# Weight remainders on GpSimd, a fourth landing buffer and a reordered first stage in a two-layer hybrid decoder

## The chip, the cores and the metric

The kernel runs on one core of a Trainium2 chip. The metric is the time of one execution on the device, in microseconds (us). TensorE (PE in the rows) multiplies matrices, VectorE (DVE), ScalarE (ACT) and GpSimd (POOL) do element-wise work, and SyncE (SP) issues most DMAs. SBUF is the on-chip working memory and PSUM holds the results of matmuls.

## The reference

Two layers (DEPTH = 2) over 512 positions of width 1024. Each layer normalises its input, scales and shifts it with a conditioning vector, and multiplies it with one wide input matrix. Two token mixers use the result: a sparse attention with 128 selected keys per query, and a chunked state-space scan. Both are projected, merged by gates, multiplied with an output matrix and added to the input.

```python
def _layer(x, c, w_ada, b_ada, norm_g, w_in, ...):
    mod = jax.nn.silu(c) @ w_ada + b_ada
    shift, scale, gate = jnp.split(mod, 3, axis=-1)
    h = _rmsnorm(x, norm_g) * (1.0 + scale[:, None, :]) + shift[:, None, :]
    proj = h @ w_in
    ...
    y_att = (o_att * jax.nn.silu(g_att)) @ w_branch_a
    ...
    y_ssd = y @ w_branch_s
    merged = jax.nn.sigmoid(gl_att) * y_att + jax.nn.sigmoid(gl_ssd) * y_ssd
    return x + gate[:, None, :] * (merged @ w_out)
```

All of it is fp32.

## The kernel before

**Weights in two parts.** TensorE works on the type fp32r here, which keeps fewer bits than fp32, so every operand of the large products is split: a rounded part `hi` and a remainder `lo = value - hi`. A product is three matmuls: hi by hi, hi by lo and lo by hi. Class `W` streams the weights in tiles of 128x1024 (some 128x936 or 128x512). `W.load` issues the DMA from SP into a landing buffer `raw`, of which there are RAWB = 3. `W.split` casts `raw` to `whi` on ScalarE (L194) and subtracts on VectorE to get the remainder `wlo` (L195). There are WB = 3 pairs of `whi` and `wlo`. `W.get` keeps AHEAD = 3 tiles split in front of the one in use and asks for RAWB more loads. There are 130 such tiles in the execution.

Some entries of the same stream are tiles of the conditioning matrix (`ada`). They land in `raw` too, and `ada_block` (L149) multiplies them on VectorE with the conditioning vector `cb` and sums along the rows. All VectorE instructions stand in one queue and run in order.

**The first stage.** `x` comes in four pieces. VectorE and ScalarE square it, and TensorE sums the squares over the channels with matmuls on a constant (`mones`, L301) into two PSUM tiles, one for each half of the 512 positions. Then `pre0(k)` runs for the eight channel tiles k = 0 to 7 of `tok_section`. For k = 0, half by half, it forms the reciprocal root (L263 to L267), then `h` (L312 on VectorE), its rounded part `hh` (L313 on ScalarE) and its remainder `hl` (L315 on VectorE). For each further k it adds two `ada` tiles (L149, for the scale and the shift), `h` and `hl` over all positions, and the split of one weight tile. `chain` ties the VectorE instructions of this stage into one fixed row.

`tok_section` runs, for each k, four blocks of 128 positions times a weight tile: three matmuls for the key and index columns (468 wide, the K part) and three for the query columns (512 wide, the Q part, one step later).

**The later stages.** The key part is rotated (`rope_k`) while the Q part ends. Then `block` multiplies weight tiles with `hh` and `hl` over all 512 positions, 24 matmuls to a tile, while other work is interleaved by generators: the index scores and the selection of keys, the scan (`ssd`), and attention. GpSimd has little to do: 16 multiplications of 128x768 in `ssd` (L715) and some DMAs, among them the loading of `x` for the residual (L881) and its saving between the layers (L912). In `out_step` the output product runs in two halves of the positions, and the second layer's `hh` and `hl` are made from the first half while the second half is still multiplied. The second layer's K part is then run for blocks 0 and 1, and after that for blocks 2 and 3.

The order within each engine's queue comes from the tile framework, which places instructions by their priority as their inputs are expected; `tc.high_priority(W_PRIO)` moves the split forward. A queue is strictly in order: what stands behind a waiting instruction waits too.

Of the kernel before, what the change touches and what calls it, by code (L numbers as in the profile page):

```python
# [12 lines left out]
AF = mybir.ActivationFunctionType  # L13
OP = mybir.AluOpType
# [4 lines left out]
KT = D // 128  # L19
# [14 lines left out]
LAG = 1  # L34
# [5 lines left out]


W_PRIO = 2000
RAWB = 3
TMPB = 7
WB = 3
AHEAD = 3
# [1 line left out]
MG_PRIO = 2300  # L48
P_ACT = 1
WARM = 1  # L50
ORDER = "s0 s1 s2 s3 T b0 b1 b2 b3 x0 x1 x2 x3 x4 x5 x6 x7 I S g0 g1 z0 z1 g2 z2 z3 g3 z4 z5 g4 z6 z7 g5 N0 g6 g7"
R_INDEX = 1
R_TOPK_X = 0.1
# [9 lines left out]
def trunk(ctx, tc, x, c, wk, wq, wt, wa, ada, pk, cst, out):  # L63
# [15 lines left out]
    def scratch(dt=F32):  # L79
        return tmp.tile([128, 512], dt, name="tmp", tag="tmp", bufs=TMPB)  # L80
# [7 lines left out]
    def raw(ap):  # L88
        return ap.bitcast(F32)
# [66 lines left out]
    class W:  # L156
        def __init__(self):
            self.src, self.loaded, self.ready, self.cb = [], {}, {}, None
            self.late, self.extra, self.keep, self.ahead = 10 ** 9, None, {}, AHEAD

        def add(self, ap, n):
            self.src.append((ap, n, None))
# [12 lines left out]
                sp.dma_start(r[:, :n], ap)  # L175
                self.loaded[i] = r

        def split(self, i, link=lambda ins: None):
            if i in self.ready:
                return  # L180
            self.load(i)
            _, n, mod = self.src[i]
            r = self.loaded[i]
            if mod is not None:
                ada_block(*mod, self.cb, r)
                self.ready[i] = None
                return
            if i in self.keep:
                hi, lo = self.keep[i]
            else:  # L190
                hi = wp.tile([128, 1024], F32R, name="whi", tag="whi", bufs=WB)
                lo = wp.tile([128, 1024], F32R, name="wlo", tag="wlo", bufs=WB)
            with tc.high_priority(W_PRIO):
                act.copy(hi[:, :n], r[:, :n])  # L194
                link(dve.tensor_sub(lo[:, :n], r[:, :n], raw(hi[:, :n])))  # L195
            self.ready[i] = (hi, lo)

        def get(self, i):
# [51 lines left out]
    def block(i, n, rh, rl, out, cols=slice(0, L)):  # L250
        hi, lo = w.get(i)
        for k in range(n):
# [4 lines left out]
            if k % 2:  # L257
                yield

    def rstd_from(r, sums, count, newton, link=lambda ins: None):  # L260
        n = r.shape[-1]
        if newton:
            act.activation(r, sums, AF.Abs_reciprocal_sqrt, bias=epst, scale=-2.0)  # L263
            t = scratch()[:, :n]
            act.activation(t, r, AF.Square)
            link(dve.scalar_tensor_tensor(t, sums, -0.5 * EPS, t, op0=OP.add, op1=OP.mult))
            link(dve.scalar_tensor_tensor(r, t, 1.5, r, op0=OP.add, op1=OP.mult))  # L267
# [25 lines left out]
    for k in range(0, KT, 2):  # L293
        if k < 4:
            in_row(act.activation(*silu[k // 2], AF.Silu))
        sq, sq1 = scratch(), scratch()
        in_row(act.activation(sq, xt[:, k], AF.Square))
        chain(dve.tensor_mul(sq1, xt[:, k + 1], xt[:, k + 1]))
        chain(dve.tensor_add(sq, sq, sq1))
        for cols, s in zip(HALVES, sums):  # L300
            pe.matmul(s, mones, sq[:, cols], start=k == 0, stop=k == KT - 2)  # L301
    pool.dma_start(cbs[:], cb[:1])
    for l in range(DEPTH):
        chain(dve.scalar_tensor_tensor(gb[l], par(l, P_BA + 8, 8), 1.0, par(l, P_NG, 8), op0=OP.add, op1=OP.mult))
# [14 lines left out]
    for l in range(DEPTH):  # L319
# [42 lines left out]
            w.ahead = 1  # L362
        accK = [bank(t) for t in BK.split()]

        def tok_section(parts, blocks, pre):
            got = {}
            for step in range(KT + max(p[3] for p in parts)):
                if step < KT:
                    pre(step)
                for i, (ids, n, acc, lag) in enumerate(parts):  # L370
                    k = step - lag
                    if not 0 <= k < KT:
                        continue
                    if k % 2 == 0:
                        got[i] = w.get(ids[k // 2])
                    a, b = (t[:, k % 2 * n:(k % 2 + 1) * n] for t in got[i])
                    for t in blocks:
                        ts = slice(t * 128, (t + 1) * 128)
                        pe.matmul(acc[t][:, :n], hh[:, k, ts], a, start=k == 0, stop=False)  # L379
                        pe.matmul(acc[t][:, :n], hh[:, k, ts], b, start=False, stop=False)  # L380
                        pe.matmul(acc[t][:, :n], hl[:, k, ts], a, start=False, stop=k == KT - 1)  # L381
                yield

        def pre0(k):
            if k == 0:
                for cols, s in zip(HALVES, sums):
                    rstd_from(rst[:, cols], s, D, True, chain)
                    h = make_h(0, k, cols, chain)
                    next(h)
                    if cols.start == 0:  # L390
                        w.split(ids0[0], chain)
                        w.load(ids0[3])
                    for _ in h:
                        pass
            else:
                h = make_h(0, k, slice(0, L), chain)
                next(h)
            if k + 1 < KT:
                ada_block(0, 9 + k, cb, aws[2 * k + 3], chain)
            for _ in h:  # L400
                pass
            if k + 1 < KT:
                ada_block(0, k + 1, cb, aws[2 * k + 2], chain)
                w.split(ids0[k + 1], chain)
                if k + 4 < KT:
                    w.load(ids0[k + 4])
                    load_ada(k + 4)

        if l == 0:
            accQ = [bank(t) for t in BQ.split()]  # L410
            rest = tok_section([(ids_k[0], NKS, accK, 0), (ids_q, 512, accQ, LAG)], range(NB), pre0)
# [597 lines left out]
```

## Time and profile before

| | us |
|---|---|
| median of 3 runs | 924.59 (923.75 to 925.49) |
| the profiled execution | 926.5 |
| span of its trace | 924.7 |
| TensorE busy | 906.5 (98%) |
| VectorE busy | 703.9 (76%) |
| ScalarE busy | 521.0 (56%) |
| GpSimd busy | 49.6 (5%) |

The span goes from the first to the last instruction; 1.8 us of the profiled execution lie around it. Busy time of TensorE counts modelled ends of pipelined matmuls, so 98% does not say that every matmul starts as early as it could: how far apart the matmuls start is read from the timeline. The granted clock of TensorE has two levels, 1.2 and 2.4 GHz, and stands in the rows as a share of the higher one.

### The profile page before, as it was taken

How to read it: one execution, taken by the hardware profiler on the slowest of the kernel's cores; microseconds unless marked ns; L12 is line 12 of the kernel's file. 1: busy time of each engine (PE TensorE's matmuls, PEld its weight loads, DVE VectorE, ACT ScalarE, POOL GpSimd, SP SyncE). 2: the span in 40 equal slices, each digit the busy share in tenths (PEclk: the TensorE clock that was granted, in tenths of full speed). 3: DMA queues.
4: the chain of work that ended last, by engine and by line, in shares of the span. 5: the costliest groups of instructions: out<-in, count | busy, mean ns of one | idle time of the engine just before them, and what ended most of it. 6: DMA issues, size and time to landing. Idle time of an engine off the chain costs nothing.

```text
span 924.7 us, 13016 instructions
## 1 busy us (share of the span) xinstructions
PE 906.5 (98%) x4780; PEld 743.8 (80%) x4780; DVE 703.9 (76%) x1384; ACT 521.0 (56%) x946; POOL 49.6 (5%) x53
## 2 busy tenths in 40 slices
PE   8999999999999999999999999999999999999996
PEld 4887788888887877777998878888888878778895
DVE  7987999999775765678497699999984675455834
ACT  5457894386265754535365588745653775463433
POOL 0000110031000000000000001102210000000000
PEclk8999999999999999999999999999999999999999
DMA  9832433232346432687344225234323532334502
GB/s 357 317 114 69 164 111 103 103 137 84 102 139 200 138 133 72 220 282 266 96 134 140 89 93 180 94 98 131 125 66 117 169 117 91 92 122 149 207 24 91
DMA packets 40609, 128.05 MB, mean 138 GB/s; under 512 B 4417, under 2 KB 6721, under 8 KB 40546
## 3 DMA queue, kind: packets, MB, share of 16 engines
q1 hardware_dynamic: 36162, 111.43, 36.6%
q0 software_dynamic: 4384, 15.80, 4.9%
q8 instruction: 37, 0.61, 0.3%
q14 instruction: 26, 0.21, 0.1%
HBM read 118.76 MB, written 8.46 MB: 138 GB/s over the span
## 4 chain that ended last, share of the span: by engine, by line
PE 88%; DVE 5%; DMA 4%; ACT 1%; issue 1%; SPq 0%; DVEq 0%; ACTq 0%
PE mm L254 21%; PE mm L255 21%; PE mm L256 21%; PE av L826 2%; PE tr L821 2%; DMA raw<-ada 2%; DVE wlo L195 1%; PE qk L723 1%; PE mm L379 1%; PE mm L381 1%; PE mm L380 1%; PE qk L798 1%; PE qk L799 1%; DMA raw<-wt 1%; PE av L740 1%
## 5 line engine op out<-in xcount | busy, mean ns | idle before, releaser
L254 PE MATMUL mm<-H,whi 128*128 128x512 f32 x640 | 258.6, 404 | 0.0
L256 PE MATMUL mm<-H,wlo 128*128 128x512 f32 x640 | 251.4, 393 | 0.0
L255 PE MATMUL mm<-H,whi 128*128 128x512 f32 x640 | 251.2, 393 | 0.0
L195 DVE TENSOR_TENSOR wlo<-raw,whi 128x1024 fp32r<-128x1024 f32 (+2 forms) x130 | 158.0, 1215 | 56.6 <-ACT whi L194 54.7
L194 ACT CAST whi<-raw 128x1024 fp32r<-128x1024 f32 (+2 forms) x130 | 130.3, 1003 | 113.1 <-PE mm L255 84.7
L254 PEld LDWEIGHTS mm<-H,whi 128*128 128x128 f32 x640 | 120.6, 188 | 26.3 <-issue 3.9
L256 PEld LDWEIGHTS mm<-H,wlo 128*128 128x128 f32 x640 | 120.5, 188 | 25.6 <-issue 0.3
L255 PEld LDWEIGHTS mm<-H,whi 128*128 128x128 f32 x640 | 120.7, 189 | 24.4 <-issue 1.9
L581 DVE MAX8 m<-B 128x8 f32<-128x256 f32 (+2 forms) x96 | 53.1, 554 | 1.2
L603 DVE SCALAR_TENSOR_TENSOR tmp<-mm,prm,tmp 128x511 f32<-128x511 f32 (+2 forms) x72 | 52.8, 736 | 0.0
L582 DVE MATCH_REPLACE8 B<-m,B 128x256 f32<-128x256 f32 (+2 forms) x96 | 52.0, 541 | 0.0
L254 PE MATMUL mm<-X,whi 128*128 128x512 f32 x128 | 51.6, 403 | 0.0
L256 PE MATMUL mm<-X,wlo 128*128 128x512 f32 x128 | 50.2, 392 | 0.3 <-DVE wlo L195 0.3
L803 ACT ACTIVATE S<-S,mx 128x128 f32<-128x128 f32 (+3 forms) x64 | 35.5, 556 | 25.3 <-DVE mx L801 25.2
L149 DVE SCALAR_TENSOR_TENSOR raw<-raw,KI 128x1024 f32<-128x1024 f32 x20 | 24.5, 1223 | 31.5 <-DMA raw<-ada 31.4
L712 ACT ACTIVATE X<-X,acs 128x128 f32<-128x128 f32 x128 | 40.5, 390 | 0.1
L255 PE MATMUL mm<-G,whi 128*128 128x512 f32 x96 | 37.7, 393 | 0.2 <-DVE G L870 0.2
L254 PE MATMUL mm<-S,A 128*128 128x256 f32 x128 | 36.9, 289 | 0.0
L256 PE MATMUL mm<-S,C 128*128 128x256 f32 x128 | 36.2, 283 | 0.0
L898 DVE SCALAR_TENSOR_TENSOR X<-mm,mod,X 128x256 f32<-128x256 f32 (+1 forms) x24 | 13.7, 571 | 28.5 <-PE mm L256 28.5
L822 ACT COPY B<-tr 128x512 f32<-128x512 f32 x40 | 22.7, 583 | 20.9 <-PE tr L821 20.6
L715 POOL TENSOR_TENSOR S<-S,G 128x768 f32<-128x768 f32 x16 | 31.1, 1954 | 60.8 <-ACT G L604 31.2
(269 smaller groups left out, 1766.0 us busy)
## 6 DMA issues: line engine op xcount, KB each, us to landing
raw<-wt SPq DMA_DIRECT2D x103, 512.0 KB, 3.5
raw<-ada SPq DMA_DIRECT2D x20, 512.0 KB, 3.9
X<-AD POOLq DMA_DIRECT2D x16, 512.0 KB, 4.4
raw<-wk SPq DMA_DIRECT2D x12, 468.0 KB, 3.4
B<-ada SPq DMA_DIRECT2D x9, 512.0 KB, 4.4
raw<-wq SPq DMA_DIRECT2D x8, 512.0 KB, 3.9
gsave<-tmp SPq DMA_DIRECT2D x16, 256.0 KB, 2.4
tmp<-gsave SPq DMA_DIRECT2D x16, 256.0 KB, 4.0
```

The lines of the kernel that those rows point to most:

```text
L149: link(dve.scalar_tensor_tensor(w, w, 1.0, cb, op0=OP.mult, op1=OP.mult, accum_out=m))
L194: act.copy(hi[:, :n], r[:, :n])
L195: link(dve.tensor_sub(lo[:, :n], r[:, :n], raw(hi[:, :n])))
L254: pe.matmul(out, h, rh[:, k, cols], start=k == 0, stop=False)
L255: pe.matmul(out, h, rl[:, k, cols], start=False, stop=False)
L256: pe.matmul(out, lw, rh[:, k, cols], start=False, stop=k == n - 1)
L581: dve.max(m8, sc)
L582: dve.match_replace(sc, m8, sc, GONE)
L603: dve.scalar_tensor_tensor(cc[:, i:], p[:, :L - i], cw(3 - i), cc[:, i:], op0=OP.mult, op1=OP.add)
L712: act.activation(ab[:, h, i], ab[:, h, i], AF.Relu, scale=-1.0, bias=acs[:, 2 * kt + h, i:i + 1])
L715: pool.tensor_tensor(cs_, cs_, BC[:, 2 + g, 128:].rearrange("p (c l) -> p c l", c=3)[:, None] .to_broadcast([128, 2, 3, 128]), op=OP.mult)
L803: act.activation(PP[:, e, :n], PP[:, e, :n], AF.Exp, bias=mx[:, e:e + 1], scale=-1.0, accum_out=sums_[:, e:e + 1])
```

## The change

- Every remainder `wlo` is subtracted on GpSimd instead of VectorE, and `W.lows` remembers the instruction. The three kinds of tiles, 128x1024, 128x936 and 128x512, all move.
- RAWB goes from 3 to 4: a fourth landing buffer.
- `rstd_from` is divided into `root` (the two ScalarE steps) and `corrected` (the two VectorE steps). In `pre0(0)` both halves' roots come first, then both halves' `h`, then both remainders `hl`.
- In `tok_section` the three matmuls of a block are no longer next to each other. First all blocks run on the rounded weights, with `hh` and `hl`, then all blocks run on the remainder. For k = 0 the row is fixed with dependencies that cost no wait.
- Behind the sums three matmuls on a tile of ones, 128x512 and fp32, run into a bank that nobody reads (IDLE = 3).
- The four DMAs that load `x` for the residual stand in GpSimd's queue behind the remainder of the last branch tile (`a7`).

```diff
-RAWB = 3
+RAWB = 4
+IDLE = 3
...
                 act.copy(hi[:, :n], r[:, :n])
-                link(dve.tensor_sub(lo[:, :n], r[:, :n], raw(hi[:, :n])))
+                self.lows[i] = pool.tensor_sub(lo[:, :n], r[:, :n], raw(hi[:, :n]))
...
-            pe.matmul(s, mones, sq[:, cols], start=k == 0, stop=k == KT - 2)
+            summed = pe.matmul(s, mones, sq[:, cols], start=k == 0, stop=k == KT - 2)
+    for i in range(IDLE):
+        made = pe.matmul(warm.rearrange("p (a b) -> p a b", a=4), ones, ones[:, None, :].to_broadcast([128, 4, 128]),
+                         start=True, stop=True)
+        tc.add_manual_dep(made.ins, summed.ins.name, NOSYNC)
+        summed = made
...
-                        pe.matmul(acc[t][:, :n], hh[:, k, ts], a, start=k == 0, stop=False)
-                        pe.matmul(acc[t][:, :n], hh[:, k, ts], b, start=False, stop=False)
-                        pe.matmul(acc[t][:, :n], hl[:, k, ts], a, start=False, stop=k == KT - 1)
+                        for h in (hh, hl):
+                            made = pe.matmul(acc[t][:, :n], h[:, k, ts], a, start=k == 0 and h is hh, stop=False)
...
+                    for t in blocks:
+                        pe.matmul(acc[t][:, :n], hh[:, k, t * 128:(t + 1) * 128], b, start=False, stop=k == KT - 1)
...
-                for cols, s in zip(HALVES, sums):
-                    rstd_from(rst[:, cols], s, D, True, chain)
-                    h = make_h(0, k, cols, chain)
+                sides = [(rst[:, cols], s) for cols, s in zip(HALVES, sums)]
+                ts = [root(*side) for side in sides]
+                hs = [make_h(0, k, cols, chain) for cols in HALVES]
+                for side, t, h in zip(sides, ts, hs):
+                    corrected(*side, t, chain)
...
-            pool.dma_start(xt[:, 2 * j:2 * j + 2], x[:, 2 * j:2 * j + 2] if l == 0 else xsave[:, 2 * j:2 * j + 2])
+            made = pool.dma_start(xt[:, 2 * j:2 * j + 2], x[:, 2 * j:2 * j + 2] if l == 0 else xsave[:, 2 * j:2 * j + 2])
+            tc.add_manual_dep(made.ins, w.lows[ids_m["a7"]].ins.name, NOSYNC)
```

What this does to the queues is seen in the order of the built programs. Numbers in the names tell buffers apart; line numbers are those of the kernel that the row belongs to.

VectorE before, from the first `h` of the first stage to the middle of step 1 (`H0` and `H1` hold `hh` and `hl`; `C` and `S` hold `ada` tiles; `G1` is `cb`):

```order
L312 SCALAR_TENSOR_TENSOR tmp_191<-X_85,gsc0_116,rst_120 128x256
L195 TENSOR_TENSOR wlo_195<-raw_166,whi_194 128x936
L315 SCALAR_TENSOR_TENSOR H1_164<-tmp_191,mod0_114,H0_163 128x256
L266 SCALAR_TENSOR_TENSOR tmp_202<-tr_123,tmp_202 128x256
L267 SCALAR_TENSOR_TENSOR rst_120<-tmp_202,rst_120 128x256
L312 SCALAR_TENSOR_TENSOR tmp_206<-X_85,gsc0_116,rst_120 128x256
L315 SCALAR_TENSOR_TENSOR H1_164<-tmp_206,mod0_114,H0_163 128x256
L149 SCALAR_TENSOR_TENSOR C_80,mod0_114<-C_80,G1_76 128x1024 x2
L195 TENSOR_TENSOR wlo_215<-raw_168,whi_214 128x1024
L312 SCALAR_TENSOR_TENSOR tmp_234<-X_85,gsc0_116,rst_120 128x512
```

Every step has one remainder of a weight tile in VectorE's row. The same piece of VectorE's queue after:

```order
L324 SCALAR_TENSOR_TENSOR tmp_197<-X_85,gsc0_116,rst_120 128x256
L269 SCALAR_TENSOR_TENSOR tmp_193<-tr_123,tmp_193 128x256
L270 SCALAR_TENSOR_TENSOR rst_120<-tmp_193,rst_120 128x256
L324 SCALAR_TENSOR_TENSOR tmp_208<-X_85,gsc0_116,rst_120 128x256
L327 SCALAR_TENSOR_TENSOR H1_167<-tmp_197,mod0_114,H0_166 128x256
L327 SCALAR_TENSOR_TENSOR H1_167<-tmp_208,mod0_114,H0_166 128x256
L150 SCALAR_TENSOR_TENSOR C_80,mod0_114<-C_80,G1_76 128x1024 x2
L324 SCALAR_TENSOR_TENSOR tmp_237<-X_85,gsc0_116,rst_120 128x512
```

The remainders are gone from VectorE and the halves of k = 0 are interleaved. They stand in GpSimd's queue, here from the first stage on, after:

```order
L197 TENSOR_TENSOR wlo_201<-raw_169,whi_200 128x936
L197 TENSOR_TENSOR wlo_218<-raw_171,whi_217 128x1024
L197 TENSOR_TENSOR wlo_246<-raw_175,whi_245 128x936
L197 TENSOR_TENSOR wlo_286<-raw_204,whi_285 128x1024
L197 TENSOR_TENSOR wlo_326<-raw_221,whi_325 128x936
L197 TENSOR_TENSOR wlo_366<-raw_249,whi_365 128x1024
L197 TENSOR_TENSOR wlo_402<-raw_289,whi_401 128x936
L197 TENSOR_TENSOR wlo_438<-raw_329,whi_437 128x1024
```

These eight belong to the first stage, which gave GpSimd nothing to do before.

TensorE after, from the end of the sums to the K part's pass on the remainder for k = 0:

```order
L308 MATMUL tr_123<-tmp_148,mones_103 128x256
L310 MATMUL mm_108<-ones_94 128x512 x3
L392 MATMUL qk_181<-whi_200,H0_166 128x468
L392 MATMUL qk_181<-whi_200,H1_167 128x468
L392 MATMUL qk_182<-whi_200,H0_166 128x468
L392 MATMUL qk_182<-whi_200,H1_167 128x468
L392 MATMUL mm_183<-whi_200,H0_166 128x468
L392 MATMUL mm_183<-whi_200,H1_167 128x468
L392 MATMUL mm_184<-whi_200,H0_166 128x468
L392 MATMUL mm_184<-whi_200,H1_167 128x468
L399 MATMUL qk_181<-wlo_201,H0_166 128x468
```

Before, the second matmul of the K part already took the remainder `wlo`; now it is the ninth, and the second takes `hl` (`H1`).

## Rows read from the trace of the kernel before

**Rows 1.** The page, parts 1 and 2: busy time, and TensorE's granted clock.
```profile
PE 906.5 (98%) x4780; PEld 743.8 (80%) x4780; DVE 703.9 (76%) x1384; ACT 521.0 (56%) x946; POOL 49.6 (5%) x53
PEclk8999999999999999999999999999999999999999
```

**Rows 2.** Windows: stretch, PE, PEld, DVE, ACT, POOL busy (instructions), granted clock, DMA share, GB/s.
```profile
15.00:20.00 5.00, 3.65 (x8) 2.58 (x9) 4.32 (x9) 2.74 (x5) 0.00 (x0) 0.60 1.03 414
20.00:25.00 5.00, 5.00 (x18) 3.99 (x17) 5.00 (x9) 2.38 (x5) 0.00 (x0) 0.71 0.93 332
...
40.00:45.00 5.00, 5.00 (x24) 4.27 (x24) 5.00 (x9) 2.05 (x4) 0.00 (x0) 1.00 1.03 402
...
285.00:290.00 5.00, 5.00 (x18) 4.01 (x18) 3.58 (x12) 3.16 (x10) 0.00 (x0) 0.66 0.45 115
...
480.00:485.00 5.00, 5.00 (x25) 4.42 (x24) 5.00 (x10) 3.87 (x11) 0.00 (x0) 1.00 0.67 201
```

**Rows 3.** Timeline, first stage: start, duration, engine, line, operation [idle before <-releaser].
```profile
12.92 0.59 PE L301 MATMUL tr<-tmp,mones 128*128 128x256 f32 x2
...
15.13 0.48 DVE L312 SCALAR_TENSOR_TENSOR tmp<-X,gsc,rst 128x256 f32<-128x256 f32 x1
...
16.35 0.76 PE L379 MATMUL qk<-whi,H 128*128 128x468 f32 x1 [2.83 <-ACT H L313]
...
19.44 1.22 DVE L149 SCALAR_TENSOR_TENSOR C<-C,G 128x1024 f32<-128x1024 f32 x1
...
20.39 0.59 PE L379 MATMUL mm<-whi,H 128*128 128x468 f32 x1
...
20.78 0.59 PE L380 MATMUL mm<-wlo,H 128*128 128x468 f32 x1
```

**Rows 4.** Timeline of VectorE, one step of the first stage.
```profile
41.15 1.22 DVE L195 TENSOR_TENSOR wlo<-raw,whi 128x1024 fp32r<-128x1024 f32 x1
42.29 0.74 DVE L312 SCALAR_TENSOR_TENSOR tmp<-X,gsc,rst 128x512 f32<-128x512 f32 x1
...
45.91 1.12 DVE L195 TENSOR_TENSOR wlo<-raw,whi 128x936 fp32r<-128x936 f32 x1
```

**Rows 5.** Timeline, end of the first stage: VectorE's last remainder, TensorE's last steps.
```profile
53.30 0.75 DVE L315 SCALAR_TENSOR_TENSOR H<-tmp,mod,H 128x512 fp32r<-128x512 f32 x1 [0.85 <-ACT H L313]
...
54.40 0.37 PE L379 MATMUL qk<-whi,H 128*128 128x468 f32 x1
...
56.96 0.40 PE L379 MATMUL tr<-whi,H 128*128 128x512 f32 x1
...
62.46 0.46 PE L466 MATMUL qk<-identr,B 128*128 128x128 f32 x4
```

**Rows 6.** Timeline, GpSimd's multiplications and VectorE's instructions beside them.
```profile
186.81 3.67 POOL L715 TENSOR_TENSOR S<-S,G 128x768 f32<-128x768 f32 x2
...
188.39 3.19 DVE L195 TENSOR_TENSOR wlo<-raw,whi 128x1024 fp32r<-128x1024 f32 x1
...
202.05 1.83 POOL L715 TENSOR_TENSOR S<-S,G 128x768 f32<-128x768 f32 x1 [0.18 <-ACT S L709]
...
202.62 0.73 DVE L747 SCALAR_TENSOR_TENSOR C<-C,prm,av 128x512 f32<-128x512 f32 x1
```

**Rows 7.** Timeline, start of attention in the first layer.
```profile
277.42 0.33 SPq L175 DMA_DIRECT2D raw<-ada  x1
...
282.84 1.23 DVE L149 SCALAR_TENSOR_TENSOR raw<-raw,KI 128x1024 f32<-128x1024 f32 x1 [2.91 <-DMA raw<-ada]
...
284.33 0.33 PE L798 MATMUL qk<-KK,A 128*128 128x128 f32 x1 [2.02 <-DVE mx L801]
```

**Rows 8.** Chain that ended last, in order of time: start, duration, link.
```profile
10.85 0.85 PE av L301 x2
...
418.44 9.18 DMA raw<-wt
...
427.70 1.05 ACT A L194
```

More of the change, by code (lines that the diff above doesn't have):

```diff
@@ L159, in __init__ @@
             self.late, self.extra, self.keep, self.ahead = 10 ** 9, None, {}, AHEAD
+            self.lows = {}
         def add(self, ap, n):
@@ L176, in load, with split @@
                 self.loaded[i] = r
-        def split(self, i, link=lambda ins: None):
+        def split(self, i):
             if i in self.ready:
@@ L258, in block, with root, corrected @@
                 yield
+    def root(r, sums):
+        act.activation(r, sums, AF.Abs_reciprocal_sqrt, bias=epst, scale=-2.0)
+        t = scratch()[:, :r.shape[-1]]
+        act.activation(t, r, AF.Square)
+        return t
+    def corrected(r, sums, t, link=lambda ins: None):
+        link(dve.scalar_tensor_tensor(t, sums, -0.5 * EPS, t, op0=OP.add, op1=OP.mult))
+        link(dve.scalar_tensor_tensor(r, t, 1.5, r, op0=OP.add, op1=OP.mult))
     def rstd_from(r, sums, count, newton, link=lambda ins: None):
-        n = r.shape[-1]
         if newton:
[L263 to L267, printed above, removed]
+            corrected(r, sums, root(r, sums), link)
         else:
@@ L363, in trunk, with tok_section @@
         accK = [bank(t) for t in BK.split()]
-        def tok_section(parts, blocks, pre):
+        def tok_section(parts, blocks, pre, row=None):
             got = {}
@@ L378, in tok_section @@
                         ts = slice(t * 128, (t + 1) * 128)
-                        pe.matmul(acc[t][:, :n], hh[:, k, ts], a, start=k == 0, stop=False)
-                        pe.matmul(acc[t][:, :n], hh[:, k, ts], b, start=False, stop=False)
-                        pe.matmul(acc[t][:, :n], hl[:, k, ts], a, start=False, stop=k == KT - 1)
+                        for h in (hh, hl):
+                            made = pe.matmul(acc[t][:, :n], h[:, k, ts], a, start=k == 0 and h is hh, stop=False)
+                            if k == 0 and row is not None:
+                                if row:
+                                    tc.add_manual_dep(made.ins, row[-1].ins.name, NOSYNC)
+                                if i == 0:
+                                    row.append(made)
+                    for t in blocks:
+                        pe.matmul(acc[t][:, :n], hh[:, k, t * 128:(t + 1) * 128], b, start=False, stop=k == KT - 1)
                 yield
@@ L385, in pre0 @@
             if k == 0:
-                for cols, s in zip(HALVES, sums):
-                    rstd_from(rst[:, cols], s, D, True, chain)
-                    h = make_h(0, k, cols, chain)
+                sides = [(rst[:, cols], s) for cols, s in zip(HALVES, sums)]
[3 more added lines that the diff above has]
+                    corrected(*side, t, chain)
                     next(h)
-                    if cols.start == 0:
-                        w.split(ids0[0], chain)
+                    if h is hs[0]:
+                        w.split(ids0[0])
                         w.load(ids0[3])
+                for h in hs:
                     for _ in h:
@@ L403, in pre0 @@
                 ada_block(0, k + 1, cb, aws[2 * k + 2], chain)
-                w.split(ids0[k + 1], chain)
+                w.split(ids0[k + 1])
                 if k + 4 < KT:
@@ L410, in trunk @@
             accQ = [bank(t) for t in BQ.split()]
-            rest = tok_section([(ids_k[0], NKS, accK, 0), (ids_q, 512, accQ, LAG)], range(NB), pre0)
+            rest = tok_section([(ids_k[0], NKS, accK, 0), (ids_q, 512, accQ, LAG)], range(NB), pre0, [])
             for _ in range(KT):
```

## Prediction

> **What bounds the kernel now.** I read the page first, then the windows for stretches where TensorE starts few matmuls, then the timeline of those stretches. TensorE is busy for 98% of the span, and its granted clock stands at the higher level nearly all the way [rows 1]. Where it has full clock and is fed, it starts 24 or 25 matmuls in 5 us [rows 2]. So the span is TensorE's own work plus a few holes, and a change that gives TensorE no work less can only win what is in the holes. There are three.
>
> The start: TensorE ends the sums at 13.5, the first product starts at 16.35 after 2.83 us of idling [rows 3], and the clock is then granted at 0.60 and 0.71, so that 15 to 25 hold 8 and 18 matmuls [rows 2]; two of them start 0.39 apart [rows 3]. At full clock a K part of one k is 12 matmuls in 2.56 us and a Q part 12 in 2.75, since a tile of 24 full-width matmuls takes 5.50 [rows 5]. Eight of each from 16.5 (16.35 and a little for a longer way through ScalarE, since both roots now come first) would end at 59.0. The stage ends at 62.46 [rows 5]. Hole: 3.5 us. The attention of the first layer: TensorE idles 2.02 us at 284.33 because VectorE waited 2.91 for a conditioning tile [rows 7], and the clock is at 0.66 afterwards with 18 matmuls in 5 us [rows 2], some 1.7 us lost. And 427.70: a load of 9.18 us is followed by its cast of 1.05 on the chain that ended last [rows 8]. Together these are some 8 us, and the good side ends about there.
>
> VectorE's 76% [rows 1] is an average. In the first stage and at the layer boundary it is busy 5.00 of 5 us, with about ten instructions [rows 2]: there the remainder counts. In the first stage a step of VectorE takes 4.76 us, of which the remainder is 1.14 [rows 4], while TensorE needs 2.56 + 2.75 = 5.31 per step. Before the change VectorE is thus ahead of TensorE there, though only by 0.55 us.
>
> **The remainders, in the first stage.** The change takes 1.14 us per step off VectorE and puts it on GpSimd. What it costs there no row shows. GpSimd's two-input multiplication of 128x768 takes 1.83 [rows 6]. Scaled by columns that is 2.24 for 936 and 2.45 for 1024, in the mean 2.35; the lower end is that the time doesn't grow, 1.83. I take the scaled one, as the columns set VectorE's times (1.22 for 1024, 0.74 for 512, [rows 4]).
>
> It doesn't run beside VectorE for free. At 188.39 a VectorE subtraction with both inputs in SBUF took 3.19 instead of 1.22 [rows 4, 6]: two GpSimd multiplications ran until 190.48, the second began while VectorE was already waiting, and VectorE needed 1.1 us from their end. GpSimd was not slowed (3.67 for two, 1.83 for one). A VectorE instruction with one input in PSUM took 0.73 beside GpSimd, undisturbed [rows 6]. All that VectorE does in a step of the first stage, the two `ada` tiles, `h` and `hl`, has two inputs in SBUF. These are another operation than the one that the row shows held, so the price lies between nothing and full exclusion; I take full exclusion, the row nearest in operands and size.
>
> The Trainium skill, "SBUF — State Buffer", section "Who interferes with whom", says that a VectorE instruction with two SBUF inputs contends with a GpSimd instruction that reads SBUF; it names no operation. The trace agrees for the one operation that it shows (3.19 us), and the rule speaks against this change: by it the sum below stands as it is, without it the first stage would gain 3.5 instead.
>
> Then VectorE and GpSimd share one row. From 15.13, where the first `h` starts [rows 3]: six half-width instructions at 0.48 are 2.9, two remainders 2.24 + 2.45 are 4.7, so the first `ada` pair starts at 22.7 instead of 19.44 [rows 3]. Seven steps follow, each 4.76 - 1.14 = 3.62, together 25.3, with six more remainders between them, 6 x 2.35 = 14.1. The last `hl` ends at 62.1; before it ended at 53.30 + 0.75 = 54.05 [rows 5]. A step is 5.97, longer than TensorE's 5.31, so TensorE waits. It has the same work behind that `hl` as before (54.40 to 62.46, [rows 5]): +8.0 us. At the flat price of 1.83 the row is shorter by 0.41 + 0.62 + 6 x 0.52 = 4.1, and the stage costs +3.9. With no exclusion VectorE is far ahead and TensorE sets the end: -3.5.
>
> The Trainium skill, "GPSIMD Engine Reference", section "Elementwise — side-by-side cycle accounting", gives 4497 ns for a two-input addition of 2048 fp32 columns. No run here shows it; by it 1024 columns are an estimated 2.25 us, and the first stage would cost some 1.6 us less than my +8.0.
>
> **The parts that serve the start.** Three matmuls on ones: two of 256 columns in fp32 take 0.85 [rows 8], so three of 512 take about 2.55 and reach from 13.5 to 16.1, just ahead of the first product; on TensorE they delay nothing. If they hold the clock, the half-clock stretch goes. The interleaved halves bring the `hl` of both halves after both `h`, and the pass on the remainder stands last, so a late `wlo` is wanted eight matmuls (1.7 us at 2.56 for 12) later. All three gains are inside the 3.5. If VectorE paces the stage they are worth nothing, as TensorE reaches the later wait earlier; in the forecast I set them at 0.
>
> **The layer boundary.** Six remainders cost 6 x 1.14 = 6.8 on VectorE before and 5 x 2.24 + 2.45 = 13.7 after, and VectorE is full there [rows 2], much of it with `h` and `hl` of two SBUF inputs. That is 6.8 more in the shared row; the later pass and the tile split ahead cover one tile's work, 2.56. Ends 0 and +4.2, taken at +2.0, the middle: VectorE's row there also holds instructions that read PSUM.
>
> **The fourth buffer.** The conditioning tile of 282.84 was issued at 277.42 [rows 7]. One more buffer lets it be issued a tile's turn earlier (2.56 at the least), but the buffer ahead of it is now given back by GpSimd, 1.0 to 1.2 later than by VectorE (2.24 - 1.12 or 2.45 - 1.22, [rows 4]). Some 1.4 us or more of the 2.91 are won. Ends 0 and -3.7 (2.02 idle and 1.7 of clock); taken at -2.5. At 427.70 a load issued earlier hides the cast behind the long landing: ends 0 and -1.05, taken at -1.0.
>
> **At nothing.** In the long stages (24 matmuls to a tile, 5.50 us) a remainder of 2.45 fits into GpSimd's row beside its multiplications, and three tiles are split ahead. VectorE's work there reads PSUM or has one input for the most part, and TensorE is fed already. If that cover is gone, each late remainder costs up to 1.2, the difference of the two engines. The loads of `x` that GpSimd issues now stand behind remainders; in SP's queue nothing is moved. A load on GpSimd's queue waits at most one remainder, 2.45, and its user comes a whole tile later.
>
> **Sum.** +8.0 + 2.0 - 2.5 - 1.0 = +6.5. On the profiled execution (926.5, of which 1.8 lie around the span) that is 933.0; it stands 1.9 above the median, so the median becomes 924.59 + 6.5 = 931.1. Its ends under exclusion: +3.9 + 0 - 3.7 - 1.05 = -0.9 (that is rival B) to +8.0 + 4.2 + 0 + 0 = +12.2, or 923.7 to 936.8. Its own likely range is 926 to 936.5.
>
> **Rivals.** *A, faster: the holding at 188.39 is a matter of that operation alone.* The `ada` tiles, `h` and `hl` (L149, L312, L315) are scalar_tensor_tensor, of which no row shows one held. If they run beside GpSimd at their own length, the step is 3.62 and TensorE is never waiting: -3.5 at the start, 0 at the boundary, -2.5 and -1.0 later, -7.0: 917.6, with ends at -8.3 (all of 284) and -4 (the clock stays low at the start). For it: only one kind of operation is seen held. Against it: the row that reads PSUM was free, so the operands decide.
>
> *B, about the same: exclusion, but GpSimd cheaper or fitting into VectorE's own gaps* (VectorE waits 0.85 for `hh` in [rows 5]). At the flat price +3.9 at the start, 0 at the boundary, -3.7 and -1.05: -0.9, so 923.7. It decides where a remainder costs the row no more than about 1.83 us.
>
> *C: the matmuls on ones don't hold the clock, so that part doesn't do what it says.* Under the forecast it changes nothing, as VectorE is late anyway; under A it costs 3 us and makes 920.6.
>
> **How the numbers follow.** Forecast 0.48, A with C inside it 0.34, B 0.18. 0.2% is 1.8 us, about what a measurement of this kernel can tell from no change. A is faster throughout (0.34), B is within it for 0.11 and splits the rest into 0.04 faster and 0.03 slower; the forecast is slower but for 0.03. Faster 0.38, same 0.14, slower 0.48. The range for 8 in 10 takes in A without its lowest end and the forecast without its highest: 916 to 936.5.
>
> **What would show it.** In the profile after: GpSimd's remainders at 2.2 to 2.5 us each; the VectorE instructions of 16 to 62 us longer than 1.22, 0.74 and 0.75 where GpSimd is busy; steps 5.97 apart; the stage's end at 70.5. If the steps are under 5.31 apart and the stage ends at 59 to 60, A holds and the largest term of my sum is wrong. Low granted clock between 16 and 23 speaks for C. The wait of TensorE at the first attention should shrink from 2.02 to under 0.5, and gaps of TensorE with `wlo` or `hl` as releaser should stand at the layer boundary. What would make the forecast wrong is above all that single reading at 188.39: it carries 11.5 us between the two answers.

## The result

The changed kernel takes 996.08 us in the median (992.21 to 996.38) against 924.99 before, a ratio of 1.076 (1.073 to 1.079). The forecast was 931.1, with 936.5 as the upper end: the sign was right, the size was wrong by a factor of eleven. The profiled execution takes 992.21, the fastest of the four, and its span is 990.4; the stages read from it below add up to 65.7 us, while the medians are 71.1 apart.

The page of the changed kernel, busy times and the granted clock:

```profile
PE 923.5 (93%) x4786; PEld 751.8 (76%) x4786; DVE 671.2 (68%) x1236; ACT 519.6 (52%) x946; POOL 395.6 (40%) x201
PEclk8999899999998999998999999999999999999999
```

TensorE has fallen from 98% to 93% [rows 1]. VectorE has 148 instructions less (1384 - 1236; the execution has 148 weight tiles, and the 130 named ahead are only the largest group of them), but its busy time sank by 32.7 us only: what stayed on it became longer. The clock row shows three dips behind the first slice, where [rows 1] had none.

The groups of instructions (busy us, mean ns of one, then the idle time before them) name what became longer. The first four lines are of the changed kernel, the last three of the kernel before:

```profile
L197 POOL TENSOR_TENSOR wlo<-raw,whi 128x1024 fp32r<-128x1024 f32 (+2 forms) x130 | 308.9, 2378 | 438.9 <-ACT whi L196 430.5 <-PE mm L399 5.4 <-PE qk L487 3.0
L150 DVE SCALAR_TENSOR_TENSOR raw<-raw,KI 128x1024 f32<-128x1024 f32 x20 | 39.0, 1952 | 41.8 <-DMA raw<-ada 34.1 <-issue 7.7
L753 DVE TENSOR_TENSOR X<-X,S 128x1024 f32<-128x1024 f32 x16 | 35.2, 2212 | 4.6 <-ACT X L735 4.6
L889 DVE TENSOR_TENSOR tmp<-tmp,C 128x512 f32<-128x512 f32 x16 | 22.1, 1380 | 0.5
...
L149 DVE SCALAR_TENSOR_TENSOR raw<-raw,KI 128x1024 f32<-128x1024 f32 x20 | 24.5, 1223 | 31.5 <-DMA raw<-ada 31.4
L732 DVE TENSOR_TENSOR X<-X,S 128x1024 f32<-128x1024 f32 x16 | 19.2, 1210 | 0.0
L868 DVE TENSOR_TENSOR tmp<-tmp,C 128x512 f32<-128x512 f32 x16 | 11.0, 687 | 0.2
```

The mean of the 130 remainders in the first line, all widths together, is 2.38 us. The `ada` tiles take 1952 ns instead of 1223, the scan's product 2212 instead of 1210, the sum of the merge 1380 instead of 687. All three have both inputs in SBUF. The largest group with an input in PSUM (L624, 128x511 or narrower) keeps its 736 ns.

Where the 65.7 us between the two spans arise is read from the same instruction in both timelines:

| first or last matmul of a stage | before | after | later by |
|---|---|---|---|
| first stage ends (first rotation of the keys) | 62.5 | 68.4 | 5.9 |
| attention of layer 1 begins | 280.3 | 300.1 | 19.8 |
| attention of layer 1 ends | 384.6 | 414.4 | 29.8 |
| last sums of layer 1 | 473.0 | 507.2 | 34.2 |
| first rotation of layer 2 | 497.9 | 534.6 | 36.7 |
| attention of layer 2 begins | 730.8 | 777.3 | 46.5 |
| attention of layer 2 ends | 830.6 | 889.9 | 59.3 |
| last sums | 916.2 | 981.8 | 65.6 |

No stage is spared. The first stage, where the prediction put its largest term, holds a tenth of the loss. The waits of TensorE (us in total, times, longest) are spread in the same way:

```profile
PE qk L819 <- DVE mx L822: 13.9, 6, 5.7
PE av L542 <- DVE tmp L539: 9.0, 2, 4.5
...
PE qk L392 <- DVE H L327: 5.7, 4, 4.3
PE mm L256 <- ACT S L890: 4.7, 2, 2.3
PE mm L257 <- DVE G L891: 3.5, 2, 1.9
```

Only the third of these lines belongs to the first stage.

### The first stage after the change

The timeline of the changed kernel (start, duration, engine, line, operation):

```profile
16.23 4.82 POOL L197 TENSOR_TENSOR wlo<-raw,whi 128x936 fp32r<-128x936 f32 x2 [7.78 <-ACT whi L196]
16.58 2.27 DVE L324 SCALAR_TENSOR_TENSOR tmp<-X,gsc,rst 128x256 f32<-128x256 f32 x1
18.78 2.95 DVE L327 SCALAR_TENSOR_TENSOR H<-tmp,mod,H 128x256 fp32r<-128x256 f32 x2
21.39 1.54 PE L392 MATMUL qk<-whi,H 128*128 128x468 f32 x3 [4.31 <-DVE H L327]
...
32.86 2.59 POOL L197 TENSOR_TENSOR wlo<-raw,whi 128x1024 fp32r<-128x1024 f32 x1 [4.98 <-ACT whi L196]
33.12 2.88 DVE L324 SCALAR_TENSOR_TENSOR tmp<-X,gsc,rst 128x512 f32<-128x512 f32 x1
...
37.76 3.25 POOL L197 TENSOR_TENSOR wlo<-raw,whi 128x936 fp32r<-128x936 f32 x1 [2.31 <-ACT whi L196]
...
59.54 0.75 DVE L327 SCALAR_TENSOR_TENSOR H<-tmp,mod,H 128x512 fp32r<-128x512 f32 x1 [0.85 <-ACT H L325]
...
68.38 0.46 PE L487 MATMUL qk<-identr,B 128*128 128x128 f32 x4
```

At 16.58 a half-width `h` takes 2.27 instead of 0.48 [rows 3], because GpSimd began 0.35 earlier; the second remainder follows at once and holds the next instruction. At 33.12 `h` takes 2.88 instead of 0.74 and ends 0.55 after the remainder. At 37.76 it is GpSimd's instruction that is long, 3.25: VectorE's `ada` multiplication was running, and GpSimd waited for it. Whichever starts first keeps the other out. These are scalar_tensor_tensor, the operation of which the trace of before showed nothing.

TensorE has its first product at 16.60 and then waits 4.31 for `hl`. In windows of 5 us (TensorE, its loads, VectorE, ScalarE, GpSimd, granted clock, DMA share, GB/s):

```profile
15.00:20.00 5.00, 1.61 (x4) 0.38 (x2) 4.81 (x6) 2.99 (x6) 3.77 (x2) 0.95 1.03 414
20.00:25.00 5.00, 3.61 (x9) 3.14 (x10) 5.00 (x8) 1.33 (x3) 1.05 (x1) 0.50 1.03 412
```

The matmuls on ones keep the clock at 0.95 in the first window, where it was 0.60 [rows 2]; the wait that follows costs it again, 0.50 in the second.

### Three places behind the first stage

The chain that forms the scan's step sizes, beside the selection of keys in layer 1:

```profile
106.19 2.34 POOL L197 TENSOR_TENSOR wlo<-raw,whi 128x1024 fp32r<-128x1024 f32 x1 [4.41 <-ACT whi L196]
106.43 2.19 DVE L536 TENSOR_TENSOR tmp<-tmp 128x64 f32<-128x64 f32 x1
110.24 0.69 PE L542 MATMUL av<-ctab,tmp 128*64 128x128 f32 x2 [4.49 <-DVE tmp L539]
```

An instruction of 64 columns takes 2.19 us, and it stands in a chain of small steps on which the next matmul waits; before, the same instruction (L515, at 101.18) took 0.21. TensorE idles 4.49 where it idled 0.17. The windows say what follows (columns as above):

```profile
105.00:110.00 5.00, 0.75 (x4) 0.29 (x2) 5.00 (x15) 3.00 (x4) 2.34 (x1) 0.83 0.07 15
110.00:115.00 5.00, 4.76 (x13) 3.54 (x14) 3.25 (x13) 1.77 (x3) 1.14 (x2) 0.50 0.26 98
```

After the idle time the clock is granted at 0.50, the lower of its two levels, and 13 matmuls start in 5 us where 24 do at full clock [rows 2]. The 11 that are missing are another 2.3 us, so by an estimate from these rows this wait is paid about one and a half times.

Start of attention in layer 1, the place of [rows 7]:

```profile
296.99 2.39 POOL L197 TENSOR_TENSOR wlo<-raw,whi 128x1024 fp32r<-128x1024 f32 x1 [5.74 <-ACT whi L196]
297.03 2.90 DVE L785 SCALAR_TENSOR_TENSOR tmp<-C,prm,tmp 128x512 f32<-128x512 f32 x1
299.86 1.21 DVE L150 SCALAR_TENSOR_TENSOR raw<-raw,KI 128x1024 f32<-128x1024 f32 x1
...
301.10 0.33 SPq L177 DMA_DIRECT2D raw<-ada  x1
...
306.26 1.23 DVE L150 SCALAR_TENSOR_TENSOR raw<-raw,KI 128x1024 f32<-128x1024 f32 x1 [4.58 <-DMA raw<-ada]
...
307.76 0.47 PE L819 MATMUL qk<-KK,A 128*128 128x128 f32 x1 [5.69 <-DVE mx L822]
```

GpSimd starts 0.04 us ahead of VectorE, and an instruction of the norm of the scan's output (L785), 0.75 us before, takes 2.90. The `ada` tile behind it is finished later, so its landing buffer comes free later and the next load is issued at 301.10. VectorE then waits 4.58 for that load, with the maximum for the softmax behind it in its queue, and TensorE idles 5.69 where it idled 2.02.

The merge of the two branches, at the end of layer 1:

```profile
451.63 2.40 POOL L197 TENSOR_TENSOR wlo<-KK,whi 128x1024 fp32r<-128x1024 f32 x1
452.27 2.32 DVE L889 TENSOR_TENSOR tmp<-tmp,C 128x512 f32<-128x512 f32 x1
...
456.29 2.36 POOL L197 TENSOR_TENSOR wlo<-raw,whi 128x1024 fp32r<-128x1024 f32 x1 [1.76 <-ACT whi L196]
456.62 2.58 DVE L889 TENSOR_TENSOR tmp<-tmp,C 128x512 f32<-128x512 f32 x1
...
459.34 5.14 POOL L197 TENSOR_TENSOR C<-raw,A 128x1024 fp32r<-128x1024 f32 x2 [0.68 <-issue]
459.90 2.35 DVE L891 SCALAR_TENSOR_TENSOR G<-tmp,S 128x512 fp32r<-128x512 f32 x1 [0.69 <-ACT S L890]
459.92 0.80 PE L256 MATMUL mm<-S,whi 128*128 128x512 f32 x1 [2.34 <-ACT S L890]
462.30 0.80 PE L257 MATMUL mm<-G,whi 128*128 128x512 f32 x1 [1.58 <-DVE G L891]
```

VectorE has only a few such instructions here and waits for ScalarE between them. But each is on the way to the next matmul, and each, of about 0.69 us, meets a remainder and takes 2.3 to 2.6.

### The profile page after: what moved, and what is told of

Read it like the earlier page. It is cut to its first block, busy times and chain, and to the rows that moved or that the text cites. A ratio compares the mean times of both kernels' runs of the same rounds, so it can differ in the third digit from the quotient of the medians.

```text
span 990.4 us, 13073 instructions
## 1 busy us (share of the span) xinstructions
PE 923.5 (93%) x4786; PEld 751.8 (76%) x4786; DVE 671.2 (68%) x1236; ACT 519.6 (52%) x946; POOL 395.6 (40%) x201
## 4 chain that ended last, share of the span: by engine, by line
PE 50%; DVE 18%; DMA 5%; ACT 4%; issue 3%; POOL 0%; DVEq 0%; SPq 0%; ACTq 0%; POOLq 0%
PE mm L257 13%; PE mm L256 13%; PE mm L258 13%; DMA raw<-ada 4%; DVE raw L150 3%; DVE B L603 1%; DVE X L753 1%; DMA B<-ada 1%; DVE m L602 1%; DVE tmp L624 1%; PE av L847 1%; DVE tmp L889 1%; DVE tmp L785 1%; PE qk L819 1%; PE qk L744 1%
## 5 line engine op out<-in xcount | busy, mean ns | idle before, releaser
L197 POOL TENSOR_TENSOR wlo<-raw,whi 128x1024 fp32r<-128x1024 f32 (+2 forms) x130 | 308.9, 2378 | 438.9 <-ACT whi L196 430.5
L256 PEld LDWEIGHTS mm<-H,whi 128*128 128x128 f32 x640 | 121.9, 191 | 32.1 <-issue 6.6
L257 PEld LDWEIGHTS mm<-H,whi 128*128 128x128 f32 x640 | 122.1, 191 | 24.7 <-issue 2.1
L150 DVE SCALAR_TENSOR_TENSOR raw<-raw,KI 128x1024 f32<-128x1024 f32 x20 | 39.0, 1952 | 41.8 <-DMA raw<-ada 34.1
L624 DVE SCALAR_TENSOR_TENSOR tmp<-mm,prm,tmp 128x509 f32<-128x509 f32 (+2 forms) x72 | 52.6, 736 | 0.1
L155 ACT ACTIVATE mod<-mod,prm 128x1 f32<-128x1 f32 x32 | 9.4, 294 | 59.0 <-DVE raw L150 34.9
L753 DVE TENSOR_TENSOR X<-X,S 128x1024 f32<-128x1024 f32 x16 | 35.2, 2212 | 4.6 <-ACT X L735 4.6
```

The lines of the kernel that those rows point to most:

```text
L150: link(dve.scalar_tensor_tensor(w, w, 1.0, cb, op0=OP.mult, op1=OP.mult, accum_out=m))
L197: self.lows[i] = pool.tensor_sub(lo[:, :n], r[:, :n], raw(hi[:, :n]))
L256: pe.matmul(out, h, rh[:, k, cols], start=k == 0, stop=False)
L257: pe.matmul(out, h, rl[:, k, cols], start=False, stop=False)
L624: dve.scalar_tensor_tensor(cc[:, i:], p[:, :L - i], cw(3 - i), cc[:, i:], op0=OP.mult, op1=OP.add)
L753: dve.tensor_mul(ab, ab, cbm[:, g][:, None].to_broadcast([128, 2, NB, 128]))
```

## The experiments

Theory 1: VectorE's instructions with two inputs in SBUF are held while GpSimd's subtraction reads SBUF, throughout the kernel. Theory 2: the remainder itself, and the landing buffer that it gives back, come late. Theory 3: the other parts of the change, or the order that the scheduler makes of it. Ratios are to the kernel before, run beside each, with 95% intervals.

**The change without GpSimd.** The remainders go back to VectorE; the fixed place of the loads of `x` behind the remainder of `a7` goes with them.

```diff
-                self.lows[i] = pool.tensor_sub(lo[:, :n], r[:, :n], raw(hi[:, :n]))
+                link(dve.tensor_sub(lo[:, :n], r[:, :n], raw(hi[:, :n])))
```

> The changed kernel with the remainders back on VectorE; the fourth buffer, the interleaved halves, the passes and the matmuls on ones stay. Theory 1 (a VectorE instruction that reads two inputs from SBUF is held whenever GpSimd's subtraction runs, in the whole kernel): without the subtractions on GpSimd nothing is held, 915 to 925 us. Theory 2 (GpSimd's remainder is late and gives its landing buffer back late, the holding costs little): also 915 to 925. Theory 3 (it is the other parts, or the order that follows from them): 970 to 995.

929.37 us, 1.0035 (1.0018 to 1.0053). It is slightly above the range of theories 1 and 2 and far from theory 3. The move to GpSimd carries 996.08 - 929.37 = 66.7 us; the rest of the change together loses a little, where the prediction let it gain.

**GpSimd without the rest.** In the kernel before, the line of the remainder alone is changed:

```diff
-                link(dve.tensor_sub(lo[:, :n], r[:, :n], raw(hi[:, :n])))
+                pool.tensor_sub(lo[:, :n], r[:, :n], raw(hi[:, :n]))
```

> The kernel before with one edit, the remainders on GpSimd. Theories 1 and 2: as slow as the changed kernel or slower, 985 to 1005 us, since the passes that put the remainder last are missing. Theory 3: 923 to 935.

996.28 us, 1.0758 (1.072 to 1.0795): the whole loss from one edit. With the remainders on GpSimd the other parts of the change, the passes among them, together neither help nor hurt (996.08). Theory 3 falls.

**The same lateness without reading SBUF.** Two kernels tell theories 1 and 2 apart. GpSimd fills the tile of the remainder instead of subtracting, once or twice:

```diff
-                self.lows[i] = pool.tensor_sub(lo[:, :n], r[:, :n], raw(hi[:, :n]))
+                pool.tensor_sub(lo[:, :1], r[:, :1], raw(hi[:, :1])); pool.memset(raw(lo[:, :n]), 0.0); self.lows[i] = pool.tensor_sub(lo[:, :1], r[:, :1], raw(hi[:, :1]))
```

> The changed kernel, but GpSimd fills the tile of the remainder with zeros instead of subtracting (the remainders are left out of the product), between two subtractions of one column that wait for the rounded part and give the landing buffer back. The order of all engines stays that of the changed kernel but for a few rows, and GpSimd hardly reads SBUF. Theory 1: VectorE is not held, 915 to 930 us. Theory 2: the tile is still finished on GpSimd behind the cast, so as far as the filling takes 1.5 to 2.5 us the time stays at 970 to 995. Theory 3: 985 to 995.

925.06 us, 0.9986 (0.9969 to 1.0003). This is the time of theory 1, but one filling is done about 1.5 us behind the cast, so theory 2 needs the second kernel.

> As gpsimd_writes_only (925.06 us), with the tile filled twice: one filling took 0.90 us and a subtraction of one column 0.30, so the remainder's tile is now finished 2 x 0.90 + 2 x 0.30 = 2.4 us behind the cast, as late as with the subtraction (2.38). The remainders are left out of the product here too. Theory 1 (VectorE is held while GpSimd reads SBUF): 920 to 930 us. Theory 2 (lateness of the remainder and of the landing buffer): back to 970 to 995.

924.88 us, 0.9997 (0.9986 to 1.0008). The page and a group of VectorE's instructions in the kernel that fills twice:

```profile
PE 903.5 (98%) x4786; PEld 742.6 (80%) x4786; DVE 554.6 (60%) x1236; ACT 519.9 (56%) x946; POOL 388.0 (42%) x645
L753 DVE TENSOR_TENSOR X<-X,S 128x1024 f32<-128x1024 f32 x16 | 19.4, 1224 | 5.9 <-ACT X L735 5.9
```

GpSimd is as busy as in the changed kernel (388.0 against 395.6), the tile is finished as late, and nothing is lost. The scan's product is back at 1224 ns. VectorE runs the same 1236 instructions in 554.6 instead of 671.2 us: the holding is 117 us. Theory 2 falls, theory 1 stands. That these kernels multiply zeros is not what makes them fast: the next one, with copies, puts full values in the same place and takes 929.75.

These two kernels say a second thing. Here the remainders cost VectorE nothing at all, and the time is that of the kernel before. Against the same kernel with the remainders on VectorE (rest_without_gpsimd, 929.37) the one that fills once is faster by 4.3 us. That is about all that taking them off VectorE could win, and it only makes up what the other parts lose. Part of it lies in the first stage, which ends at 59.69 in that kernel, against 62.46 [rows 5] before and 61.53 to 63.84 in the two kernels that have the same start with the remainders on VectorE (start_parts_only, rest_without_gpsimd):

```profile
59.69 0.46 PE L487 MATMUL qk<-identr,B 128*128 128x128 f32 x4
```

**One input instead of two.**

```diff
-                self.lows[i] = pool.tensor_sub(lo[:, :n], r[:, :n], raw(hi[:, :n]))
+                pool.tensor_copy(lo[:, :n], raw(hi[:, :n])); self.lows[i] = pool.tensor_sub(lo[:, :1], r[:, :1], raw(hi[:, :1]))
```

> The changed kernel, but GpSimd copies the rounded part into the tile of the remainder (one input from SBUF, so the product holds the rounded part twice) and gives the landing buffer back with a subtraction of one column. Theory 1a (any GpSimd instruction that reads SBUF holds VectorE's two-input instructions): VectorE's instructions are stretched by up to the copy's length, and the time is between 940 and 990, the more the longer a copy takes. Theory 1b (only GpSimd's two-input instructions hold it): 920 to 930, and none stretched.

929.75 us, 1.0058 (1.004 to 1.0076), below the range of 1a and at the upper end of 1b, so the rows decide. A copy and VectorE's instruction beside it, a group, and the page:

```profile
28.82 1.27 POOL L197 CAST wlo<-whi 128x1024 fp32r<-128x1024 f32 x1 [4.33 <-ACT whi L196]
29.13 1.52 DVE L324 SCALAR_TENSOR_TENSOR tmp<-X,gsc,rst 128x512 f32<-128x512 f32 x1
```

```profile
L753 DVE TENSOR_TENSOR X<-X,S 128x1024 f32<-128x1024 f32 x16 | 22.8, 1433 | 5.9 <-ACT X L735 5.9
PE 903.9 (98%) x4786; PEld 742.5 (80%) x4786; DVE 578.2 (62%) x1236; ACT 520.2 (56%) x946; POOL 255.3 (28%) x349
```

A copy with one input holds VectorE too (1.52 instead of 0.74). The holding is 578.2 - 554.6 = 24 us by the two pages' VectorE, and costs 4.9 us of time over the kernel that fills twice. With the subtraction 117 us of holding cost 71. So the loss per held us is larger with the long holds. That short ones fit into the slack ahead of TensorE and those of 2.4 us don't is a likely reason, but not shown. GpSimd's reading holds VectorE, with one input or two; the expectation's price for 1a was wrong.

**Where the loss lies.** Three kernels give GpSimd a part of the tiles only. The first keeps the first stage's eight on VectorE:

```diff
-                self.lows[i] = pool.tensor_sub(lo[:, :n], r[:, :n], raw(hi[:, :n]))
+                self.lows[i] = link(dve.tensor_sub(lo[:, :n], r[:, :n], raw(hi[:, :n]))) if link else pool.tensor_sub(lo[:, :n], r[:, :n], raw(hi[:, :n]))
```

> The changed kernel with the eight remainders of the first stage on VectorE, all others on GpSimd. The last hl of the first stage ended 6.2 us later after the change (60.3 against 54.05). Theory 1: the stage ends at 59 to 62 and the time falls by 5 to 9 us, to 986 to 991; the rest of the loss lies behind the first stage. If the holding mattered in the first stage alone, as the prediction had it, the time would fall to 925 to 930.

988.24 us, 1.0665 (1.0631 to 1.0699). The eight remainders of the first stage are worth 996.08 - 988.24 = 7.8, and the stage ends at 61.51. The rest of the loss lies behind it.

For the other two a tile is given to GpSimd if it is in a set, here the tiles of the gates, the convolutions and the scan:

```diff
-                self.lows[i] = pool.tensor_sub(lo[:, :n], r[:, :n], raw(hi[:, :n]))
+                self.lows[i] = link(dve.tensor_sub(lo[:, :n], r[:, :n], raw(hi[:, :n]))) if link else (pool if i in self.far else dve).tensor_sub(lo[:, :n], r[:, :n], raw(hi[:, :n]))
...
-                 for t in ORDER.split() if t[0] in base}
+                 for t in ORDER.split() if t[0] in base}; w.far |= set(ids_x.values())
```

> The changed kernel with GpSimd making only the remainders of the tiles from the conditional branches of the scan (names s, b, x, g, z in ORDER), the stretch in which VectorE was 98% busy before. Against the kernel before, the changed kernel lost 13.9 us there in the first layer and 9.8 in the second. If the losses of the stages add up: 929 + 24 = 953, from 945 to 958. If VectorE's relief pays there as the prediction's rival had it: 915 to 928.

952.97 us, 1.0298 (1.0282 to 1.0313). And here the tiles beside and after attention:

```diff
-        ids_o = [add(wt[l, 48 + j], 1024) for j in range(KT)]
+        ids_o = [add(wt[l, 48 + j], 1024) for j in range(KT)]; w.far |= set(ids_m.values()) | set(ids_o)
```

> The changed kernel with GpSimd making only the remainders of the tiles used beside and after attention (MORDER and the output matrix), where VectorE was 40 to 80% busy before. The changed kernel lost 14.4 us there in the first layer and 19.1 in the second. If the losses add up: 929 + 33 = 962, from 953 to 968. If what counts is how full VectorE is, little is lost here: 928 to 938.

964.08 us, 1.042 (1.04 to 1.0441). Both lie about where the table of stages put them. The parts add up: 7.8 + (952.97 - 929.37 = 23.6) + (964.08 - 929.37 = 34.7) = 66.1 of 66.7. The 0.6 that is left for the layer boundary is smaller than the intervals, so these runs don't show what the boundary cost. Each of the two sets has 64 remainders, and the larger loss is where VectorE was the less busy: before, it was busy for 90% and 83% of the two stages of the scan (their fullest parts are what the expectation calls 98%), and for 54 to 70% of the stages from attention on. How full VectorE is doesn't tell the loss. By the three places above it is what stands between VectorE's result and the next matmul.

**The other parts alone.** First the buffer, on the kernel before:

```diff
-RAWB = 3
+RAWB = 4
```

> The kernel before with RAWB = 4 alone. By the prediction's term for the fourth buffer (-2.5 at the first attention, -1.0 behind the long load): 921 to 923 us. By the trace of rest_without_gpsimd, where TensorE still waits 1.53 and 0.86 us at the first attention although the buffer is there: no gain, 924 to 930, and the fourth buffer may be what costs that kernel its 0.35%.

926.46 us, 1.0008 (0.9995 to 1.0021): no gain. The wait at the first attention is there, in VectorE's and SP's timelines:

```profile
276.40 1.22 DVE L149 SCALAR_TENSOR_TENSOR raw<-raw,KI 128x1024 f32<-128x1024 f32 x1
...
277.65 0.33 SPq L175 DMA_DIRECT2D raw<-ada  x1
...
283.06 1.23 DVE L149 SCALAR_TENSOR_TENSOR raw<-raw,KI 128x1024 f32<-128x1024 f32 x1 [2.48 <-DMA raw<-ada]
```

The load is issued at 277.65, against 277.42 with three buffers [rows 7], right behind the conditioning tile before it (276.40 + 1.22). One more buffer let it start no earlier; why not, the trace doesn't show. TensorE idles 1.56 there.

The matmuls on ones, on the kernel before:

```diff
-            pe.matmul(s, mones, sq[:, cols], start=k == 0, stop=k == KT - 2)
+            summed = pe.matmul(s, mones, sq[:, cols], start=k == 0, stop=k == KT - 2)
+    for i in range(IDLE):
+        made = pe.matmul(warm.rearrange("p (a b) -> p a b", a=4), ones, ones[:, None, :].to_broadcast([128, 4, 128]),
+                         start=True, stop=True)
+        tc.add_manual_dep(made.ins, summed.ins.name, NOSYNC)
+        summed = made
```

> The kernel before with the three matmuls on ones alone. If they hold the clock up to the first product: the stretch of 16 to 23 us runs at full clock and the time falls by up to 3 us, 922 to 925. If they don't: 924 to 927, with a granted clock under 0.8 in 15 to 25 us.

924.98 us, 0.9994 (0.9979 to 1.0009). The windows:

```profile
15.00:20.00 5.00, 4.07 (x15) 2.22 (x14) 4.32 (x9) 3.03 (x6) 0.00 (x0) 1.00 1.03 415
20.00:25.00 5.00, 3.05 (x11) 2.20 (x10) 5.00 (x9) 2.17 (x4) 0.00 (x0) 0.85 0.89 330
25.00:30.00 5.00, 5.00 (x20) 4.21 (x19) 5.00 (x10) 2.03 (x4) 0.00 (x0) 0.81 0.88 322
```

They do hold the clock up to 20 us. TensorE then runs ahead of VectorE and waits 1.95 us for a remainder at 23.29, and behind that wait the granted clock is low (0.85 and 0.81), one window later than before [rows 2]. Neither of the two expectations had that.

The passes, on the kernel before:

```diff
...
-                        pe.matmul(acc[t][:, :n], hh[:, k, ts], b, start=False, stop=False)
...
+                    for t in blocks:
+                        pe.matmul(acc[t][:, :n], hh[:, k, t * 128:(t + 1) * 128], b, start=False, stop=k == KT - 1)
```

> The kernel before with the K and Q parts run in passes, the remainder last, and nothing else. With the remainders on VectorE they come early enough for the old order, so the passes give nothing: 924 to 927 us, the end of the first stage within 0.5 us of 62.46. If running one block's matmuls apart costs something on TensorE, the stage ends later than 63.

927.23 us, 1.0019 (1.0004 to 1.0034); the stage ends at 62.24.

All three parts of the start, as in rest_without_gpsimd, with three buffers:

```diff
-RAWB = 4
+RAWB = 3
```

> The kernel with the interleaved halves, the passes and the matmuls on ones, with three landing buffers and the remainders on VectorE. If the fourth buffer cost rest_without_gpsimd its 0.35%: 921 to 925 us. If the parts of the start did: 927 to 930.

927.93 us, 1.0025 (1.0012 to 1.0039), not clearly apart from rest_without_gpsimd with its fourth buffer (1.0018 to 1.0053). In its profile the clock is granted at 1.00 in every window from 10 to 30 us and the first stage ends at 61.53, 0.9 us earlier than before, and yet the kernel isn't faster. In rest_without_gpsimd TensorE has the same wait at 18.52 (1.88 us against 1.89 here), but there the clock falls behind it, 0.54 from 20 to 25, and the stage ends at 63.84. With the same matmuls behind the same wait, the clock alone can thus shift the end of this stage by some 2 us. The lead is lost again behind the first stage. The scheduler's order differs there as well, and what costs the 0.2% was not found; it stays open. No kernel here beats the one before by more than its interval.

## Why the prediction was wrong

**The mechanism was right.** VectorE and GpSimd share one row wherever VectorE's instruction has two inputs in SBUF and GpSimd's reads SBUF, for scalar_tensor_tensor as for the subtraction; rival A is refuted by 16.58 and 33.12. Rival B's condition isn't met: six remainders cost VectorE's row 13.3 us between 21.65 and 60.29, 2.2 each, and not 1.83. Against rival C, the matmuls on ones hold the clock up to the first product (0.95 in the first window); it falls at the wait behind it. The Trainium skill, "SBUF — State Buffer", section "Who interferes with whom", says that a VectorE instruction with two SBUF inputs contends with a GpSimd instruction that reads SBUF and not with one that only writes it. The runs agree: 117 us of holding with reading, VectorE's two-input groups at their old length with writing alone.

**The price of a remainder was right:** for 128x1024, 2.45 forecast and 2.34 to 2.40 measured (106.19, 296.99, 451.63).

**The first stage was sized somewhat high.** The last `hl` ends at 60.29 and not at 62.1, the stage at 68.38 and not at 70.5: +5.9 in the trace (7.8 by the experiment) against +8.0. The first `ada` pair starts at 21.65 (22.7 forecast). From there to the last `hl` it is 38.6 us, against the 39.4 of the forecast (25.3 for seven steps and 14.1 for six remainders). The exclusion is not quite full: at 33.12 the held instruction ends 0.55 after the remainder, where it takes 0.74 alone.

**The layer boundary** was +2.0 with ends 0 and +4.2; it is 2.5 in the table, and the experiments don't resolve it.

**The fourth buffer** was -3.5 in sum and is nothing. The prediction took the number of buffers as the limit on the load. With three and with four the load is issued when the conditioning tile before it ends (276.40 + 1.22, issue at 277.65); why that stays so with four is open.

**The step that failed is "At nothing".** That term priced the long stages by throughput (whether GpSimd has time for 2.45 us in a tile of 5.50) and by the lateness of a remainder, "up to 1.2" each. GpSimd had the time (busy for 40%), and gpsimd_writes_twice shows that lateness costs nothing that its interval would show. The prediction didn't apply there what it had just derived for the first stage, that each remainder also holds VectorE. "VectorE's work there reads PSUM or has one input for the most part" was not counted, and where it is so the prediction was right (L624 keeps its 736 ns), but the exceptions (the step sizes, the norm of the scan's output, the `ada` tiles, the merge) are those on which TensorE waits. That term was 0 and measures 23.6 + 34.7 = 58.3 us. It is also why the range failed: the unknown that was given two ends in the first stage was given one value for the 860 us after it.

With the price that the prediction had, a bound was at hand: 140 further remainders of 2.35 are 329 us, at the most, in which a two-input instruction of VectorE can be held. Nothing in [rows 6] limited that to the first stage, and 188.39 itself lies in the scan.

## What to carry to other kernels

Moving element-wise work to an idle engine is not free if, as here, the reading of one engine holds the other: count, for every instruction that stays behind, whether it can be held, and whether a matmul waits for it. An engine's busy share says little here; the dearer holds hit VectorE where it had been idle for 30 to 46% of the time, but on the way to TensorE. And before paying for relief, ask what the relief is worth: a kernel in which VectorE did no remainder at all was no faster than the one before.

## What was not expected of the hardware

Filling from GpSimd is not entirely without effect on VectorE. In the kernel that fills twice, a tensor_scalar with one input and one output in SBUF is slowed: three of 128x384 take 2.07 us beside two fillings, and the mean of this group of 12 is 671 ns, where before it was 416.

```profile
332.57 2.06 POOL L197 MEMSET wlo<- 128x1024 f32 x2
333.10 2.07 DVE L834 TENSOR_SCALAR S<-S,sm 128x384 f32<-128x384 f32 x3
```

The two-input group L753, which reading lengthened from 1210 to 2212 ns, is at 1224 in the same kernel. So what writing does to the one kind it doesn't do to the other. The changed kernel lengthens the same instruction at other widths (128x512: 615 ns instead of 483). Why it is held was not looked into.
